# A hybrid decoder block on one core: tiles of f moved by 128 bytes, sums of squares taken on TensorE at three seams, splits of weights ordered behind the root

## The chip, the core and the metric

The kernel runs on one NeuronCore of one Trainium2 chip. The metric is the device time of one execution in microseconds; lower is better. All times below are in us unless they say ns.

## What is computed

One decoder layer over 512 tokens of width 2048, all in float32:

```python
mod = silu(c) @ w_mod + b_mod                    # six vectors: sh1 sc1 gt1 sh2 sc2 gt2
h = rmsnorm(x, g_mix) * (1 + sc1) + sh1
u, q, k, v = split(h @ w_in)                     # 2048 x 4096
y = concat(rmsnorm(s5_mixer(u)), rmsnorm(dilated_attention(q, k, v)))
x = x + gt1 * (y @ w_out)
h = rmsnorm(x, g_ffn) * (1 + sc2) + sh2
f = (silu(h @ w_gate) * (h @ w_up)) @ w_down     # inner width 5632
x = x + gt2 * f
return rmsnorm(x, g_final)

def rmsnorm(x, g):
    return x * rsqrt(mean(x * x, axis=-1) + 1e-6) * g
```

Three of these norms run over the whole width of 2048: before w_in, before w_gate and w_up, and at the end. The change touches how their sums of squares and their roots are formed, and how the last matrix product reads its moving operand.

## The kernel before

**Layout.** Activations are stored transposed, features on the 128 partitions and the 512 tokens along the free dimension, so one tile of a feature block is 128x512 float32, 2048 bytes in a partition. Every matrix product is done as three matmuls in the fp32r format (`mm3`): an operand is split into hi (a cast, on ScalarE) and lo = raw - hi (a subtraction, on VectorE), and hi*hi, hi*lo and lo*hi are accumulated. Weights come by DMA on SP's queue as pieces of 128x1024 (512 KB) into five buffers `raw`; their split goes into three buffers each of `hi` and `lo` (pool `whl`).

**Order.** The kernel is written in a tile framework: the program gives every operation in order, and a planner fixes the order on each engine before the run, from its own estimates and a priority (by default the place in the program; `tc.high_priority(30)` lets an operation go ahead). On the chip each engine, and SP's DMA queue, takes its list strictly in that order. A tile's buffer is taken again when its readers are done. `tc.issue_after(ins)` adds the order "behind ins" for operations on the engine of ins. `prog` is the list of matrix products with calls between them; background generators (`start`, `pump`) put VectorE and ScalarE work between the k steps.

**The head.** x arrives in eight DMAs. Each of its 16 tiles is squared on ScalarE and added on VectorE into `ssq` or `rbc` in turn, and the two are added. Four Silus of c, broadcast over the partitions by matmuls with `sel`, stand between the squares. `rsq_stages` makes the root: four matmuls with a column of ones sum over the partitions (a float32 matmul is two passes, so the profile shows eight), VectorE does a first guess and three Newton steps on a 128x4 tile, four matmuls broadcast the result to 128x512, and it is copied to `rbc`. Meanwhile `gv` multiplies rows of w_mod (512 KB each, eight buffers) with cb, four for each k of the modulation; `h_mod(k)` and `h_make(k)` then make the hi and lo tiles of h (hA for k below 4, hB above). The first product, `first_h` before each of its steps, starts as soon as h(0) is there.

**The seam before gate and up.** `residual(cb_, half)` adds the last quarter of y @ w_out to x1. Each tile is squared on ScalarE and added to ssq on VectorE (`sumsq4`); after the last quarter the root follows (`rsq_psum`), and `h3` makes the two operands b of the next product. `wk_prep(k)` splits the weights of its step k; the splits of k = 0 and 1 are in the program right behind the root.

**The down projection and the end.** f goes through DRAM and comes back as tiles of 128x2x512 (hi and lo beside each other) in eight buffers (pool `ft`). Two products of 44 steps each, 24 matmuls to a step, have the weights stationary and f moving. `acc(c)` adds the eight results of a product to x1 and sums squares the same way; `last` makes the root, multiplies and stores.

**Addresses.** SBUF addresses in a partition, modulo 256 bytes, by the memory map of this kernel: hA, hB, vv, ys, raw, hi, lo and st 192; b, t1 to t4 160; f 64 (114496 and on, 4096 apart). The tile `fpad` in front of `ft` has no other use than to shift it.

Of the kernel before, what the change touches and what calls it, by code (L numbers as in the profile page):

```python
# [10 lines left out]
F32 = mybir.dt.float32  # L11
F32R = mybir.dt.float32r
I32 = mybir.dt.int32
AF = mybir.ActivationFunctionType
ALU = mybir.AluOpType

P = 128
S = 512
D = 2048
KT = D // P  # L20
# [25 lines left out]
def hybrid_block(ctx: ExitStack, tc: tile.TileContext, xT, crow, vecs, pos, kc, km, w_mod, w_in, s5a, s5bc,  # L46
                 s5d, w_glu, w_out, w_gate, w_up, w_down, outT):
    nc = tc.nc
    PE, ACT, DVE, POOL, SP = nc.tensor, nc.scalar, nc.vector, nc.gpsimd, nc.sync
    tt = DVE.tensor_tensor  # L50
    stt = DVE.scalar_tensor_tensor
# [27 lines left out]
    def gps(tag="g"):  # L79
        return banks[tag].tile([P, S], F32, tag=tag, name=nm(tag))  # L80

    def mps():
        return gps("m" if "m" in banks else "g")

    def st():
        return stg.tile([P, S], F32, tag="st", name=nm("st"))
# [5 lines left out]
    bgs = []  # L92

    def start(gen, rate):
        bgs.append([gen, rate, 0.0])
        return bgs[-1]
# [16 lines left out]
    def finish(h):  # L113
        while h in bgs:
            advance(h, 1)
# [115 lines left out]
    ones = kct[:, K_ONE:K_ONE + 1]  # L231
# [3 lines left out]
    cb = const.tile([P, D], F32, name="cb")  # L235
    macc = const.tile([P, 96, 2], F32, name="macc")
    gs = const.tile([P, 16], F32, name="gs")
# [37 lines left out]
    def xf(k):  # L275
        return (vg if k < 8 else xb)[:, k % 8]
# [3 lines left out]
    crow4 = crow_sb[0:4]  # L280
# [28 lines left out]
    def gv(n):  # L309
        for _ in range(n):  # L310
            gv_loads()
            m, h = gq[gat[0]]
            raw = graw.pop(gat[0])
            stt(raw, raw, 1.0, cb[:, h * (D // 2):(h + 1) * (D // 2)], op0=ALU.mult, op1=ALU.mult,  # L314
                accum_out=macc[:, m, h:h + 1])
            gat[0] += 1
            gv_loads()
# [19 lines left out]
    def sumsq(acc, x, first):  # L337
        if first:
            ACT.activation(acc, x, AF.Square)
        else:  # L340
            t = st()
            ACT.activation(t, x, AF.Square)
            tt(acc, acc, t, op=ALU.add)

    def sumsq4(acc, xs, first):

        ts = []
        for i, x in enumerate(xs):
            ts.append(acc if first and i == 0 else st())
            ACT.activation(ts[-1], x, AF.Square)  # L350
        yield
        for t in ts:
            if t is not acc:
                tt(acc, acc, t, op=ALU.add)

    root = [None]

    def rsq_stages(out, acc, n):

        ps = mps()  # L360
        for j in range(4):
            PE.matmul(ps[:, j:j + 1], acc[:, j * P:(j + 1) * P], ones, start=True, stop=True)
        yield
        v = small.tile([P, 4], F32, tag="rv", name=nm("rv"))
        ii = small.tile([P, 4], I32, tag="ri", name=nm("ri"))
        h = small.tile([P, 4], F32, tag="rh", name=nm("rh"))
        t = small.tile([P, 4], F32, tag="rt", name=nm("rt"))
        DVE.tensor_scalar(v, ps[:, :4], 1.0 / n, EPS, op0=ALU.mult, op1=ALU.add)
        DVE.tensor_scalar(ii, v.bitcast(I32), 1, None, op0=ALU.logical_shift_right)
        DVE.tensor_scalar(ii, ii, -1, 0x5F3759DF, op0=ALU.mult, op1=ALU.add)  # L370
        DVE.tensor_scalar(h, v, -0.5, None, op0=ALU.mult)
        y = ii.bitcast(F32)
        for _ in range(3):
            tt(t, y, y, op=ALU.mult)
            tt(t, t, h, op=ALU.mult)
            stt(y, t, 1.5, y, op0=ALU.add, op1=ALU.mult)
        yield
        pb = mps()
        for j in range(4):
            PE.matmul(pb[:, j * P:(j + 1) * P], y[:, j:j + 1].to_broadcast([P, P]), ident,  # L380
                      start=True, stop=True)
        yield
        if out is None:
            root[0] = pb
        else:
            ACT.copy(out, pb)

    def rsq_psum(acc, n):
        for _ in rsq_stages(None, acc, n):
            pass  # L390
        return root[0]

# [80 lines left out]
    gv_loads()  # L473
    gb1 = const.tile([P, 16], F32, name="gb1")
    stt(gb1, vec[:, V_BMOD + SC1:V_BMOD + SC1 + 16], 1.0, vec[:, V_GMIX:V_GMIX + 16], op0=ALU.add, op1=ALU.mult)
    for i in range(KT):
        sumsq((ssq, rbc)[i % 2], xf(i), i < 2)
        if i in (3, 5, 7, 9):
            j = i // 2 - 1
            ps = gps()  # L480
            PE.matmul(ps, sel[:, j], crow4, start=True, stop=True)
            ACT.activation(cb[:, j * S:(j + 1) * S], ps, AF.Silu)
    tt(ssq, ssq, rbc, op=ALU.add)

    def h_mod(k):

# [7 lines left out]
    def h_make(k, between=None):  # L494

        made.add(k)
        hi, lo = act_h(k)
        sh = mod[:, SH1 + k:SH1 + k + 1]
        t = st()
        halves = [slice(0, S // 2), slice(S // 2, S)]  # L500
        for c in halves:
            stt(t[:, c], xf(k)[:, c], gs[:, k:k + 1], rbc[:, c], op0=ALU.mult, op1=ALU.mult)
            ACT.activation(hi[:, c], t[:, c], AF.Identity, bias=sh)
        if between is not None:
            between()
        for c in halves:
            stt(lo[:, c], t[:, c], sh, hi[:, c].bitcast(F32), op0=ALU.add, op1=ALU.subtract)
# [32 lines left out]

    def first_h(k, hi, lo):
        if k == 0:
            rs = rsq_stages(rbc, ssq, D)
            next(rs)
            gv(1)
            next(rs)
            next(rs)
            gv(3)
            h_mod(0)
            for _ in rs:  # L550
                pass
            hi()
        else:
            hi()
            gv(4)
            h_mod(k)
        h_make(k, lo)

    for i, (c0, kg) in enumerate(QK1):
        gemm(wiv, QC + c0, 0, range(kg), act_h, store([part[c0 // P + m] for m in range(8)], SP), w=2 * S,  # L560
# [359 lines left out]
    x1 = []  # L920
# [66 lines left out]
    def attention():  # L987
        with tc.tile_pool(name="att", bufs=2, side="right", reuse_waits="tile") as ap, \
# [83 lines left out]

            yield from pipe(range(4 * NH), a0, a1, a2, a2b, a3, a4, a5)

    def residual(cb_, half):
        def fn(pss):
            assert ('mod', GT1) in made
            fs_ = range(4 * cb_, 4 * cb_ + 4)
            for m, f in enumerate(fs_):
                stt(pss[m], pss[m], mod[:, GT1 + f:GT1 + f + 1], (rbc, ssa)[half], op0=ALU.mult, op1=ALU.mult)  # L1080
                if m:
                    tt(x1[0][:, f - 1], pss[m - 1], x1[0][:, f - 1], op=ALU.add)
            tt(x1[0][:, f], pss[3], x1[0][:, f], op=ALU.add)
            if half:
                SP.dma_start(x1v[:, fs_[0]:f + 1], x1[0][:, fs_[0]:f + 1])
                start(sumsq4(ssq, [x1[0][:, f] for f in fs_], cb_ == 0), 1)
                if cb_ == 3:
                    finish(bgs[-1])
        return fn

    def win5():
# [37 lines left out]
    fd = dram.tile([FF // P, P, 2 * S], F32, name="fd")  # L1129
    finish(hh[-1])  # L1130

    def hl(raw):
        hi = whl.tile([P, 2 * S], F32R, tag="hi", name=nm("hi"))
        lo = whl.tile([P, 2 * S], F32R, tag="lo", name=nm("lo"))
        ACT.copy(hi, raw)  # L1135
        tt(lo, raw, hi.bitcast(F32), op=ALU.subtract)  # L1136
        return hi, lo

    wk, wkr = {}, {}
# [10 lines left out]
                SP.dma_start(v[:, j, i], w[i, kh, :, :, kk * P:(kk + 1) * P].rearrange("f p c -> p f c"))  # L1150
        wkr[k] = t

    def wk_prep(k):
        for j in range(4):
            wk_load(k + j)
        if k < KT:
            with tc.high_priority(30):
                wk[k] = hl(wkr[k])

    for k in range(4):  # L1160
        wk_load(k)
    r = rsq_psum(ssq, D)
    wk_prep(0)
    wk_prep(1)
    yx.close()
    mrx.close()
    open_banks(g=8)
# [170 lines left out]
    def acc(c):  # L1338
        def fn(pss):
            assert ('mod', GT2) in made  # L1340
            xs = [x1[0][:, 8 * c + m] for m in range(8)]
            for m, x in enumerate(xs):
                o = GT2 + 8 * c + m
                stt(x, pss[m], mod[:, o:o + 1], x, op0=ALU.mult, op1=ALU.add)
                if m % 4 == 3:
                    start(sumsq4(ssq, xs[m - 3:m + 1], c == 0 and m == 3), 1)
                    if c == 1:
                        finish(bgs[-1])
        return fn

    gq += [(GT2 + k, h) for k in range(KT) for h in range(2)]
# [13 lines left out]
    for n, (bl, p) in enumerate(items):  # L1365
        prep(n + 2)
        if n == len(items) - 4:

            t12x.close()
            ftx.enter_context(tc.tile_pool(name="fpad", bufs=1, side="right")).tile([P, 24], F32, name="fpad")  # L1370
            fpool = ftx.enter_context(tc.tile_pool(name="ft", bufs=8, side="right", reuse_waits="tile"))
            ft.append(fpool)
            for j in range(7):
                f_load(j)
            while at[1] < 3:
                load_piece(pieces[at[1]])
                at[1] += 1
# [64 lines left out]
    def last():  # L1442
        ov = kview(outT)
        x, g = x1[0], vec[:, V_GFIN:V_GFIN + KT]
        r = rsq_psum(ssq, D)
        for k in range(KT):
            stt(x[:, k], x[:, k], g[:, k:k + 1], r, op0=ALU.mult, op1=ALU.mult)
            SP.dma_start(ov[:, k], x[:, k])
# [78 lines left out]
```

## Time and profile before

| | us |
|---|---|
| median of three runs | 2206.57 (2206.29 to 2213.41) |
| the profiled execution | 2206.05 |
| its span, first to last instruction | 2204.3 |
| first matmul of the first large product | starts at 32.68 |
| product before gate and up ends, first b matmul | 791.8 and 804.37 |
| down projection, first to last matmul | 1691.2 to 2182 |

A line of a timeline shows the start, the duration, the engine, the line of the kernel, the operation with its output and inputs, and in brackets how long the engine was idle before it and what ended that. A line of a table of stretches gives the stretch, its length, then for PE, PEld, DVE, ACT and POOL the busy time with the number of instructions, and at the end the granted TensorE clock, the share of the DMA engines and GB/s. PE is the matmuls, PEld the loading of weights beside them, DVE is VectorE, ACT is ScalarE, SPq is SP's DMA queue.

### The profile page before, as it was taken

The page shows a single profiled execution, that of the slowest core. Times are in us where ns is not written, and L with a number is a line of the kernel's source. Part 1 is how long each engine was busy: PE and PEld are TensorE (multiplying, and loading weights), DVE is VectorE, ACT ScalarE, POOL GpSimd, SP SyncE. Part 2 cuts the span into 40 slices and gives each one's busy share as a digit, 9 for nine tenths or more (in the row PEclk, how much of TensorE's full clock was granted, in tenths as well). Part 3 has the DMA queues.
Part 4 walks back from the last instruction along what each step waited for, and adds up shares of the span by engine and source line. Part 5 has one row for each costly group of instructions (what it writes and reads, how often), then busy time and mean ns, then how long its engine had stood idle before and what let it go on. Part 6 is the DMA issues. An engine that isn't in the chain of part 4 may idle for free.

```text
span 2204.3 us, 32293 instructions
## 1 busy us (share of the span) xinstructions
PE 2114.6 (96%) x12744; PEld 1870.0 (85%) x12744; DVE 1518.0 (69%) x2219; ACT 851.1 (39%) x1213; POOL 2.0 (0%) x7
## 2 busy tenths in 40 slices
PE   5999999889999989999999999999999999999996
PEld 3778787777787868999999999999999888888885
DVE  7896877976888776787887878878886443232225
ACT  3432343366653353444444444444443111121111
POOL 0000000000000000000000000000000000000000
PEclk9999989999999989999999999999999999999998
DMA  9999885678887633343343434434346888555552
GB/s 356 331 355 168 226 265 182 235 232 271 299 280 242 208 105 96 134 144 125 128 140 126 147 121 135 144 125 142 117 140 242 314 320 312 190 189 186 188 171 77
DMA packets 212047, 435.91 MB, mean 198 GB/s; under 512 B 50676, under 2 KB 87924, under 8 KB 211896
## 3 DMA queue, kind: packets, MB, share of 16 engines
q1 hardware_dynamic: 211656, 433.13, 59.3%
q8 instruction: 100, 1.64, 0.3%
q0 software_dynamic: 240, 0.72, 0.1%
q14 instruction: 51, 0.42, 0.1%
HBM read 380.38 MB, written 53.41 MB: 197 GB/s over the span
## 4 chain that ended last, share of the span: by engine, by line
PE 73%; DVE 7%; DMA 4%; issue 1%; ACT 0%; SPq 0%; DVEq 0%; ACTq 0%
PE g L191 11%; PE g L193 11%; PE g L192 11%; PE y L1395 5%; PE y L1393 5%; PE y L1394 5%; PE z L1395 3%; PE x L1395 3%; PE x L1394 3%; PE z L1394 3%; PE z L1393 3%; PE x L1393 3%; DMA mraw<-in_w_mod 3%; DVE mraw L314 1%; PE m L772 1%
## 5 line engine op out<-in xcount | busy, mean ns | idle before, releaser
L165 DVE TENSOR_TENSOR lo<-raw,hi 128x1024 fp32r<-128x1024 f32 x192 | 234.7, 1224 | 336.7 <-ACT hi L161 332.3
L161 ACT CAST hi<-raw 128x1024 fp32r<-128x1024 f32 x192 | 201.2, 1049 | 575.0 <-PE g L192 383.1
L1135 ACT CAST hi<-raw 128x1024 fp32r<-128x1024 f32 x176 | 185.2, 1052 | 290.4 <-PE x L1394 116.6
L314 DVE SCALAR_TENSOR_TENSOR mraw<-mraw,cb 128x1024 f32<-128x1024 f32 x192 | 233.0, 1222 | 80.2 <-DMA mraw<-in_w_mod 80.0
L1136 DVE TENSOR_TENSOR lo<-raw,hi 128x1024 fp32r<-128x1024 f32 x176 | 215.2, 1223 | 94.9 <-ACT hi L1135 94.8
L191 PE MATMUL g<-f,hi 128*128 128x512 f32 x704 | 277.8, 395 | 0.0
L192 PE MATMUL g<-f,hi 128*128 128x512 f32 x704 | 277.8, 395 | 0.0
L193 PE MATMUL g<-f,lo 128*128 128x512 f32 x704 | 277.8, 395 | 0.0
L1135 ACT CAST hi<-s 128x1024 fp32r<-128x1024 f32 x120 | 126.3, 1052 | 165.8 <-PE y L1394 82.6
L1394 PE MATMUL x<-b,hi 128*128 128x256 f32 x640 | 179.8, 281 | 0.0
L1393 PE MATMUL y<-t,hi 128*128 128x256 f32 x640 | 179.8, 281 | 0.0
L1395 PE MATMUL x<-b,lo 128*128 128x256 f32 x640 | 179.8, 281 | 0.0
L1394 PE MATMUL y<-t,hi 128*128 128x256 f32 x640 | 179.8, 281 | 0.0
L1395 PE MATMUL y<-t,lo 128*128 128x256 f32 x640 | 179.8, 281 | 0.0
L1393 PE MATMUL x<-b,hi 128*128 128x256 f32 x640 | 179.8, 281 | 0.0
L191 PEld LDWEIGHTS g<-f,hi 128*128 128x128 f32 x704 | 132.6, 188 | 31.0
L192 PEld LDWEIGHTS g<-f,hi 128*128 128x128 f32 x704 | 132.6, 188 | 30.9
L193 PEld LDWEIGHTS g<-f,lo 128*128 128x128 f32 x704 | 132.6, 188 | 30.9
L1136 DVE TENSOR_TENSOR lo<-s,hi 128x1024 fp32r<-128x1024 f32 x120 | 146.4, 1220 | 16.8 <-ACT hi L1135 16.3
L191 PE MATMUL g<-hB,hi 128*128 128x512 f32 x288 | 115.6, 403 | 12.6 <-DVE rt L883 12.5
L1394 PEld LDWEIGHTS x<-b,hi 128*128 128x128 f32 x640 | 120.6, 188 | 0.0
L1393 PEld LDWEIGHTS x<-b,hi 128*128 128x128 f32 x640 | 120.6, 188 | 0.0
(312 smaller groups left out, 4928.5 us busy)
## 6 DMA issues: line engine op xcount, KB each, us to landing
mraw<-in_w_mod SPq DMA_DIRECT2D x192, 512.0 KB, 6.1
raw<-in_w_down SPq DMA_DIRECT2D x88, 512.0 KB, 4.1
f<-fd SPq DMA_DIRECT2D x88, 512.0 KB, 3.9
raw<-in_w_gate SPq DMA_DIRECT2D x80, 512.0 KB, 3.3
raw<-in_w_up SPq DMA_DIRECT2D x80, 512.0 KB, 3.7
raw<-in_w_in SPq DMA_DIRECT2D x64, 512.0 KB, 5.4
fd<-fo SPq DMA_DIRECT2D x40, 512.0 KB, 4.4
raw<-in_w_out SPq DMA_DIRECT2D x32, 512.0 KB, 5.5
```

The source lines that it names most:

```text
L161: ACT.copy(hi, p["raw"])
L165: tt(p["hl"][1], p["raw"], p["hl"][0].bitcast(F32), op=ALU.subtract)
L191: PE.matmul(ps, lhs[0], rhs[0], start=first, stop=False)
L192: PE.matmul(ps, lhs[0], rhs[1], start=False, stop=False)
L193: PE.matmul(ps, lhs[1], rhs[0], start=False, stop=last)
L314: stt(raw, raw, 1.0, cb[:, h * (D // 2):(h + 1) * (D // 2)], op0=ALU.mult, op1=ALU.mult, accum_out=macc[:, m, h:h + 1])
L772: PE.matmul(d["pi"][:, i * NJ:(i + 1) * NJ], d["pm"][i // 4][:, i % 4], Ug[:, 8 * c + i], start=True, stop=True)
L1135: ACT.copy(hi, raw)
L1136: tt(lo, raw, hi.bitcast(F32), op=ALU.subtract)
L1393: PE.matmul(o, hi[:, sl], bh[:, k], start=f, stop=False, skip_group_check=True)
L1394: PE.matmul(o, hi[:, sl], bo[:, k], start=False, stop=False, skip_group_check=True)
L1395: PE.matmul(o, lo[:, sl], bh[:, k], start=False, stop=l, skip_group_check=True)
```

## The change

In the head the four Silus come ahead of the squares; one square in four is done on VectorE; four tiles' squares are added into a tile of their own, and this tile goes to TensorE's sum over partitions (`ssq_mm`), which accumulates the four groups in one PSUM tile. The root is taken ahead of the four products of w_mod for k = 0, which are put behind the last Newton step; h(0) reads the root from PSUM, and the copy to `rbc` comes after h(0). In `residual` and `acc` the last two squares skip the add into ssq and go to TensorE by themselves. The lo parts of the split weights for k = 0 and 1 are put behind the last add to x1 and behind the last Newton step. `fpad` has 56 floats in place of 24.

```diff
-    def rsq_stages(out, acc, n):
-
-        ps = mps()
+    chain = [None]
+    def ssq_mm(ps, x, first, last):
         for j in range(4):
-            PE.matmul(ps[:, j:j + 1], acc[:, j * P:(j + 1) * P], ones, start=True, stop=True)
+            PE.matmul(ps[:, j:j + 1], x[:, j * P:(j + 1) * P], ones, start=first and j == 0, stop=last,
+                      skip_group_check=True)
+    def rsq_stages(out, acc, n, ps=None):
+        if ps is None:
+            ps = mps()
+            for j in range(4):
+                PE.matmul(ps[:, j:j + 1], acc[:, j * P:(j + 1) * P], ones, start=True, stop=True)
...
-            stt(y, t, 1.5, y, op0=ALU.add, op1=ALU.mult)
+            chain[0] = stt(y, t, 1.5, y, op0=ALU.add, op1=ALU.mult)
...
+        root[0] = pb
         yield
-        if out is None:
-            root[0] = pb
-        else:
+        if out is not None:
             ACT.copy(out, pb)
...
+    psx = gps()
+    for j in range(4):
+        ps = gps()
+        PE.matmul(ps, sel[:, j], crow4, start=True, stop=True)
+        ACT.activation(cb[:, j * S:(j + 1) * S], ps, AF.Silu)
     for i in range(KT):
-        sumsq((ssq, rbc)[i % 2], xf(i), i < 2)
-        if i in (3, 5, 7, 9):
-            j = i // 2 - 1
-            ps = gps()
-            PE.matmul(ps, sel[:, j], crow4, start=True, stop=True)
-            ACT.activation(cb[:, j * S:(j + 1) * S], ps, AF.Silu)
-    tt(ssq, ssq, rbc, op=ALU.add)
+        q = st()
+        if i % 4 == 2:
+            tt(q, xf(i), xf(i), op=ALU.mult)
+        else:
+            ACT.activation(q, xf(i), AF.Square)
+        if i % 4:
+            tt(acc4, acc4, q, op=ALU.add)
+        else:
+            acc4 = q
+        if i % 4 == 3:
+            ssq_mm(psx, acc4, i == 3, i == KT - 1)
...
-            stt(t[:, c], xf(k)[:, c], gs[:, k:k + 1], rbc[:, c], op0=ALU.mult, op1=ALU.mult)
+            stt(t[:, c], xf(k)[:, c], gs[:, k:k + 1], (rbc if k else root[0])[:, c], op0=ALU.mult, op1=ALU.mult)
...
         if k == 0:
-            rs = rsq_stages(rbc, ssq, D)
+            rs = rsq_stages(rbc, None, D, psx)
+            with tc.high_priority(30):
+                next(rs)
+                next(rs)
             next(rs)
-            gv(1)
-            next(rs)
-            next(rs)
-            gv(3)
+            with tc.issue_after(chain[0].ins):
+                gv(4)
             h_mod(0)
-            for _ in rs:
-                pass
             hi()
...
         h_make(k, lo)
+        if k == 0:
+            for _ in rs:
+                pass
...
             if half:
+                x1_done[:] = [done]
                 SP.dma_start(x1v[:, fs_[0]:f + 1], x1[0][:, fs_[0]:f + 1])
-                start(sumsq4(ssq, [x1[0][:, f] for f in fs_], cb_ == 0), 1)
-                if cb_ == 3:
-                    finish(bgs[-1])
+                if cb_ < 3:
+                    sq.append(start(sumsq4(ssq, [x1[0][:, f] for f in fs_], cb_ == 0), 1))
+                    return
+                for h in sq:
+                    finish(h)
+                psq.append(mps())
+                ts = []
+                for f in fs_:
+                    ts.append(st())
+                    ACT.activation(ts[-1], x1[0][:, f], AF.Square)
+                for t in ts[:2]:
+                    tt(ssq, ssq, t, op=ALU.add)
+                for i, t in enumerate((ssq, *ts[2:])):
+                    ssq_mm(psq[0], t, i == 0, i == 2)
...
+        with tc.issue_after(after.ins) if after is not None else nullcontext():
+            tt(lo, raw, hi.bitcast(F32), op=ALU.subtract)
...
-    r = rsq_psum(ssq, D)
-    wk_prep(0)
-    wk_prep(1)
+    with tc.high_priority(30):
+        r = rsq_psum(None, D, psq[0])
+    wk_prep(0, x1_done[0])
+    wk_prep(1, chain[0])
...
-                if m % 4 == 3:
-                    start(sumsq4(ssq, xs[m - 3:m + 1], c == 0 and m == 3), 1)
-                    if c == 1:
-                        finish(bgs[-1])
+                if c == 0:
+                    if m % 4 == 3:
+                        start(sumsq4(ssq, xs[m - 3:m + 1], m == 3), 1)
+                else:
+                    ts.append(st())
+                    ACT.activation(ts[m], x, AF.Square)
+                    if m < 6:
+                        tt(ssq, ssq, ts[m], op=ALU.add)
+            if c == 1:
+                psq[0] = mps()
+                for i, t in enumerate((ssq, *ts[6:])):
+                    ssq_mm(psq[0], t, i == 0, i == 2)
...
-            ftx.enter_context(tc.tile_pool(name="fpad", bufs=1, side="right")).tile([P, 24], F32, name="fpad")
+            ftx.enter_context(tc.tile_pool(name="fpad", bufs=1, side="right")).tile([P, 56], F32, name="fpad")
```

More of the change, by code (lines that the diff above doesn't have):

```diff
@@ L381, in rsq_stages, with rsq_psum @@
                       start=True, stop=True)
+        root[0] = pb
         yield
-        if out is None:
-            root[0] = pb
-        else:
+        if out is not None:
             ACT.copy(out, pb)
-    def rsq_psum(acc, n):
-        for _ in rsq_stages(None, acc, n):
+    def rsq_psum(acc, n, ps=None):
+        for _ in rsq_stages(None, acc, n, ps):
             pass
@@ L1073, in attention @@
             yield from pipe(range(4 * NH), a0, a1, a2, a2b, a3, a4, a5)
+    sq, psq, x1_done = [], [], []
     def residual(cb_, half):
@@ L1082, in fn @@
                     tt(x1[0][:, f - 1], pss[m - 1], x1[0][:, f - 1], op=ALU.add)
-            tt(x1[0][:, f], pss[3], x1[0][:, f], op=ALU.add)
+            done = tt(x1[0][:, f], pss[3], x1[0][:, f], op=ALU.add)
             if half:
+                x1_done[:] = [done]
                 SP.dma_start(x1v[:, fs_[0]:f + 1], x1[0][:, fs_[0]:f + 1])
-                start(sumsq4(ssq, [x1[0][:, f] for f in fs_], cb_ == 0), 1)
-                if cb_ == 3:
-                    finish(bgs[-1])
+                if cb_ < 3:
[12 more added lines that the diff above has]
+                    ssq_mm(psq[0], t, i == 0, i == 2)
         return fn
@@ L1130, in hybrid_block, with hl @@
     finish(hh[-1])
-    def hl(raw):
+    def hl(raw, after=None):
         hi = whl.tile([P, 2 * S], F32R, tag="hi", name=nm("hi"))
@@ L1135, in hl @@
         ACT.copy(hi, raw)
-        tt(lo, raw, hi.bitcast(F32), op=ALU.subtract)
+        with tc.issue_after(after.ins) if after is not None else nullcontext():
+            tt(lo, raw, hi.bitcast(F32), op=ALU.subtract)
         return hi, lo
@@ L1151, in wk_load, with wk_prep @@
         wkr[k] = t
-    def wk_prep(k):
+    def wk_prep(k, after=None):
         for j in range(4):
@@ L1157, in wk_prep @@
             with tc.high_priority(30):
-                wk[k] = hl(wkr[k])
+                wk[k] = hl(wkr[k], after)
     for k in range(4):
         wk_load(k)
-    r = rsq_psum(ssq, D)
-    wk_prep(0)
-    wk_prep(1)
+    with tc.high_priority(30):
+        r = rsq_psum(None, D, psq[0])
+    wk_prep(0, x1_done[0])
+    wk_prep(1, chain[0])
     yx.close()
@@ L1341, in fn @@
             xs = [x1[0][:, 8 * c + m] for m in range(8)]
+            ts = []
             for m, x in enumerate(xs):
@@ L1444, in last @@
         x, g = x1[0], vec[:, V_GFIN:V_GFIN + KT]
-        r = rsq_psum(ssq, D)
+        r = rsq_psum(None, D, psq[0])
         for k in range(KT):
```

## The prediction

> **What bounds the kernel now.** I read the page's busy list first, then the busy time of stretches that hold only matmuls, then the chain of work that ended last at the two late root computations, then the order of time in the first 60 us.
>
> ```profile
> span 2204.3 us, 32293 instructions
> PE 2114.6 (96%) x12744; PEld 1870.0 (85%) x12744; DVE 1518.0 (69%) x2219; ACT 851.1 (39%) x1213; POOL 2.0 (0%) x7
> ...
> 120.00:220.00 100.00, 100.00 (x442) 82.79 (x442) 78.05 (x175) 28.49 (x39) 1.20 (x2) 1.00 0.99 249
> 840.00:880.00 40.00, 40.00 (x173) 32.21 (x172) 20.52 (x14) 12.47 (x11) 0.00 (x0) 1.00 0.34 105
> 1700.00:1900.00 200.00, 200.00 (x862) 162.13 (x861) 82.72 (x102) 37.75 (x36) 0.00 (x0) 1.00 0.84 298
> 1940.00:2140.00 200.00, 200.00 (x863) 162.13 (x862) 45.22 (x38) 37.72 (x36) 0.00 (x0) 1.00 0.57 192
> ...
> L191 PE MATMUL g<-f,hi x704: 390/393/404, 1691.2 to 2181.3; 128*128 128x512 f32 x176
> ```
>
> TensorE is busy 96% of the span, so time can come from two places only: a shorter step between matmuls, or a shorter hole. The four stretches have PE full at a granted clock of 1.00, and their matmuls stream 512 columns. A matmul that straddles an edge is counted on both sides, so I take one off each count: 100/441 = 0.2268 us where hA and hB are streamed, 40/172 = 0.2326 for b, 200/861 = 0.2323 and 200/862 = 0.2320 in f's two halves. The share of the DMA engines (next to last column) is 0.99 in the quick stretch, and f's pace is the same at 0.84 and at 0.57: traffic is not the reason. The f row gives the pace over the whole stage: 703 triples between its first and last start, 490.1 us, so 5.577 us for the 24 matmuls of one k.
>
> **Term A, the tiles of f.** The pad in front of them grows from 24 to 56 floats, so they move 128 bytes down, from 64 to 192 modulo 256. In the kernel's memory map hA, hB, vv and ys stand at 192, the weights' hi and lo also, b at 160. The gemm over vv has the shape of the down projection (weights stationary, 512 contiguous floats moving); its pace is the distance of two splits, each of which follows the matmuls of one k:
>
> ```profile
> 775.36 1.05 ACT L161 CAST hi<-raw 128x1024 fp32r<-128x1024 f32 x1 [2.65 <-PE g L192]
> 780.80 1.05 ACT L1135 CAST hi<-raw 128x1024 fp32r<-128x1024 f32 x1 [4.39 <-DMA raw<-in_w_up]
> ```
>
> That is 5.44 us, and 24 x 0.2268 gives 5.44 as well. If f at 192 runs as these do, 88 steps (704 triples, 8 to a step) save 88 x (5.577 - 5.44) = 12.1 us. Nothing else holds the stage: PE has no hole in it, and the DMA share of 0.84 would rise to 0.86. Bounds: 12.1 (no row is quicker than 5.44) and nothing (the offset is not the cause); a loss is priced among the rivals. I take 12.1, since every 512-column tile at 192 has that pace. [...]
>
> **Term B, the root before the gate and up projections.** The last matmul, then the chain of waits:
>
> ```profile
> 791.43 0.39 PE L193 MATMUL g<-vv,lo 128*128 128x512 f32 x1
> ...
> 791.40 1.23 DVE lo L1136
> 792.63 0.67 DVE g L1080
> 793.80 0.69 DVE x L1083
> 794.49 1.13 DVE lo L1136
> 795.62 0.61 DVE ssq L354
> 796.37 1.85 PE m L362 x8
> 800.73 2.06 PE m L380 x8
> 802.81 0.76 DVE st L1185
> 803.60 0.73 ACT b L1188
> 804.37 0.79 PE g L191
> ...
> 794.52 0.63 ACT L350 ACTIVATE st<-x 128x512 f32<-128x512 f32 x1 [1.70 <-DVE x L1083]
> ...
> 578.72 0.79 PE m L362 x8
> ...
> 586.04 0.89 PE m L380 x8
> ```
>
> Two splits (lo) stand in this chain ahead of the root, and an add into ssq follows the last square. The change holds the split of k = 0 until x1 is done, that of k = 1 until the Newton chain is done, and gives the last two squares to TensorE directly. New sum from the last matmul's end at 791.82: g 0.67, x 0.69, square 0.63 and 0.1 of hand-over make 793.9. The sums over ssq and the third square run meanwhile, behind the last matmul: 8 passes cost 0.79 on a busy PE (row 578.72), two sets end at 793.4, so both are hidden; at the cold price of 1.85 they would end at 795.5. The set for the last square costs 0.79 to 1.85; I take 1.05, which the same work took 2.3 us after the last matmul in the tail (below): 795.0. Newton's 2.5 (796.37 + 1.85 to 800.73) makes 797.5, the broadcast 2.06, st 0.76, b 0.73: first matmul 801.1 instead of 804.37, so 3.3. The split of k = 0 lies under the square and the sum (1.1 of 1.8 us), that of k = 1 under the broadcast (1.1 of 2.06); uncovered each costs 1.13. The split of k = 2 has no such edge and can still slip in ahead of Newton, so I take 3.0. Bounds: all three sets cold, 791.82 + 3 x 1.85 = 797.4 against 798.2, gain 0.8; the last set at 0.79, gain 3.6. On SP the store of x1 waits for x1 and has loads of weights behind it; both come earlier, and those weights are for k of 2 and more, 11 us on.
>
> [...]
>
> **Term C, the last root.**
>
> ```profile
> 2181.92 0.25 PE g L193
> 2182.19 0.76 DVE x L1344
> 2183.04 0.64 ACT st L350
> 2183.70 0.70 DVE ssq L354
> 2184.45 1.07 PE g L362 x8
> 2187.93 2.09 PE g L380 x8
> ```
>
> The add (0.70 and 0.05 of hand-over) goes. The sets for ssq and the seventh square run from 2182.17: at 0.79 they end at 2183.75, just when the eighth square is there (2183.70), and the whole 0.75 plus 0.28 of a warmer last set is won; at 1.07 they end at 2184.3 and 0.15 is left. Taken: 0.7. The sixteen outputs behind it stay.
>
> **Term D, the head.**
>
> ```profile
> 3.63 7.19 PE L481 MATMUL g<-st,st 4*128 4x512 f32 x8 [3.63 <-DVE st L469]
> 15.16 3.23 ACT L342 ACTIVATE st<-xb 128x512 f32<-128x512 f32 x6
> 18.85 0.68 DVE L343 TENSOR_TENSOR rbc<-rbc,st 128x512 f32<-128x512 f32 x1
> 20.71 4.19 SPq L305 DMA_DIRECT2D mraw<-in_w_mod  x3
> 21.34 1.87 PE L362 MATMUL g<-kct,ssq 128*128 128x1 f32 x8 [10.51 <-DVE ssq L483]
> 27.91 2.08 PE L380 MATMUL g<-kct,ri 128*128 128x128 f32 x8 [4.71 <-DVE ri L376]
> 30.06 1.22 DVE L314 SCALAR_TENSOR_TENSOR mraw<-mraw,cb 128x1024 f32<-128x1024 f32 x1
> 31.21 0.48 DVE L502 SCALAR_TENSOR_TENSOR st<-vg,gs,rbc 128x256 f32<-128x256 f32 x1
> 32.68 0.79 PE L191 MATMUL g<-hA,hi 128*128 128x512 f32 x1 [2.69 <-ACT hA L503]
> 43.70 0.79 PE L193 MATMUL g<-hA,lo 128*128 128x512 f32 x1 [2.68 <-DVE lo L165]
> 51.27 1.23 DVE L165 TENSOR_TENSOR lo<-raw,hi 128x1024 fp32r<-128x1024 f32 x1 [3.02 <-ACT hi L161]
> ```
>
> All four Silus now stand ahead of the squares; the broadcast they read ends at 10.8, so ACT may start its 12 squares at 11.4 and end them at 18.3 (0.57 each), as before (18.4). DVE has 16 operations at 0.60 in place of 15, and its last add ends between 17.5 (x streams in freely) and 21.5 (nothing of it done before 11.4); taken 19.5. Then sums 1.87, Newton 2.5, and only then the four products with w_mod, 4 x 1.15, and 0.4 of small ones: h(0) starts at 28.9 instead of 31.21, and the first matmul 2.3 earlier. But DVE is the bound here, and before the change two more products and a split (3.45 us) were done by 31.21. With them it is 32.3, so DVE runs 1.1 late, and the next wait of PE, at 43.70, is for DVE: what is won at k = 0 is waited out at k = 1. What DVE loses meets its 3.02 us of idling at 51.27. SP reloads w_mod 4 to 5 us later than 20.71, with w_in behind; eight products' worth of tiles is in flight by then, which covers it to about 26. PSUM: the root's bank, read by h(0) directly, is freed by the copy to rbc one step later, before the eighth bank is asked for. Bounds: 3 won, 3 lost; taken: 0.5 won.
>
> **Sum.** 12.1 + 3.0 + 0.7 + 0.5 = 16.3 us off the profiled execution's 2206.05 (1.75 more than its span; 0.52 below the median of the runs, 2206.57): 2189.8.
>
> **Rivals.**
> 1. *The offset does not matter to f* (its tiles are DMA-written, which hA and vv are not). For it: b at 160 and f at 64 differ by 0.1% only. Against: weights, which feed the same matmuls, never change. 2206.05 - 4.2 = 2201.9; Chance 0.10. [...]
> 2. *The head loses.* stg has five buffers; if each group's sum tile is handed on only after its PE sums, a group takes 1.87 + 0.57 + 3 x 0.60 = 4.2 us in series, the last add ends at 14.3 + 12.7 = 27.0, h(0) starts at 36.4, 5.2 late. 2189.8 + 0.5 + 5.2 = 2195.5. Against: two tiles free up at 10.8 and leave all five. Chance 0.11.
> 3. *192 is the wrong residue for f*: moving operand and weights then start alike, and f has eight tiles where vv has one block. Price from the 256-column matmuls at 160:
>
> ```profile
> 960.00:1000.00 40.00, 40.00 (x340) 40.00 (x339) 32.39 (x37) 18.11 (x23) 0.00 (x0) 1.00 0.40 133
> ```
>
> 40/339 = 0.1180 each, 0.2360 for 512 columns, 5.66 us for a step: 88 x 0.087 = 7.6 lost, 2206.05 + 7.6 - 4.2 = 2209.5, slower. It decides from 5.625 us for a step on. Against: hA to ys, all alike with the weights. Chance 0.04.
> 4. *PE stays warm at the seam of term B*: the broadcast 1.2 shorter, eight matmuls at 0.23 in place of 0.43 (1.6): 2187.0. Against: the tail's 2.09. Chance 0.08. [...]
>
> **Numbers.** My forecast keeps 0.67. About 0.3% (6.6 us) is what a measurement of this kernel can tell from no change. Faster by more than that (below 2199.4): forecast, rival 4 and nearly all of rival 2, 0.85; within: rival 1 and the near part of rival 3, 0.12; slower 0.03. Range: below, 2189.8 - 2.5 (head) - 1.1 (B and C at their best) - 2.2 (most of rival 4) = 2184; above, rival 2 with B at its lower bound, 2195.5 + 2.2 = 2197.7, 2198. It leaves out rivals 1 and 3.
>
> **What would show it.** Right: the f row spans 478 to 479 us, with mean durations of 389 to 391 ns; the first b matmul starts 9.5 us after the last vv matmul's end in place of 12.6; the last Newton chain follows the square without an add. Wrong: an f step of 5.58 (rival 1) or above 5.62 (rival 3); a PE wait in the first 60 us longer than those at 32.68 and 43.70 together; a split between x1 and Newton.

## The result and the profile after

| | before | after |
|---|---|---|
| median of the runs | 2206.43 (2206.13 to 2213.41, four runs) | 2189.8 (2189.05 to 2192.96, four runs) |
| profiled execution, its span | 2206.05, 2204.3 | 2189.05, 2187.2 |

The ratio is 0.9914, with an interval of 0.9895 to 0.9933. The comparison leaves out disturbed runs.

The busy list of the kernel after, then its stretches that hold only matmuls (columns as before), then the row of f:

```profile
span 2187.2 us, 32392 instructions
PE 2109.8 (96%) x12800; PEld 1874.8 (86%) x12800; DVE 1516.8 (69%) x2216; ACT 849.6 (39%) x1209; POOL 2.0 (0%) x7
```

```profile
840.00:880.00 40.00, 40.00 (x173) 32.20 (x172) 16.19 (x12) 9.16 (x9) 0.00 (x0) 1.00 0.34 105
1700.00:1900.00 200.00, 200.00 (x884) 165.59 (x883) 81.34 (x101) 39.04 (x37) 0.00 (x0) 1.00 0.86 301
```

```profile
L191 PE MATMUL g<-f,hi x704: 389/389/396, 1686.5 to 2164.5; 128*128 128x512 f32 x176
```

TensorE holds f's stretch without a gap as before, but with 884 matmuls in place of 862: 200/883 = 0.2265 us. The f row spans 478.0 in place of 490.1; over its 703 triples that is 0.2266 a matmul in place of 0.2324. The gemm over b, which was not moved, is at 173 in its 40 us as before.

The seam before gate and up, on TensorE's timeline and then in the chain of waits:

```profile
788.86 0.39 PE L193 MATMUL g<-vv,lo 128*128 128x512 f32 x1
789.08 0.95 PE L362 MATMUL m<-kct,ssq 128*128 128x1 f32 x8
789.89 1.03 PE L362 MATMUL m<-kct,st 128*128 128x1 f32 x8
791.49 1.05 PE L362 MATMUL m<-kct,st 128*128 128x1 f32 x8 [0.56 <-ACT st L1116]
795.06 2.04 PE L388 MATMUL m<-kct,ri 128*128 128x128 f32 x8 [2.52 <-DVE ri L384]
798.79 0.79 PE L191 MATMUL g<-b,hi 128*128 128x512 f32 x1 [1.68 <-ACT b L1222]
```

```profile
790.08 0.70 DVE x L1103
790.80 0.64 ACT st L1116
791.49 1.07 PE m L362 x8
795.15 0.95 issue
796.10 1.22 DVE lo L1169
797.32 0.67 DVE st L1219
```

From the last matmul's end (789.25) to the first b it is 9.54 in place of 12.55. The two sums that need not wait stand right behind the last matmul, the third follows the last square, and a split appears in the chain only behind the Newton steps (lo at 796.10, which runs beside the broadcast and ends 0.2 behind it: 797.32 against 795.06 + 2.04).

The tail, TensorE's timeline, then ScalarE's last square:

```profile
2164.98 0.39 PE L193 MATMUL g<-f,lo 128*128 128x512 f32 x1
2165.45 1.05 PE L362 MATMUL g<-kct,ssq 128*128 128x1 f32 x8
2166.37 1.93 PE L362 MATMUL g<-kct,st 128*128 128x1 f32 x16
2170.73 2.08 PE L388 MATMUL g<-kct,ri 128*128 128x128 f32 x8 [2.43 <-DVE ri L384]
```

```profile
2166.25 0.63 ACT L1385 ACTIVATE st<-x 128x512 f32<-128x512 f32 x1 [0.73 <-DVE x L1379]
```

Three sets now run in a row, 2.85 us from 2165.45, in place of a single one behind an add. From the start of the last matmul the span ends 22.22 us later, before the change 22.52 (2204.27 - 2181.76). In the experiments below it is 22.09 to 22.45 with this tail.

The head, first TensorE, then VectorE:

```profile
20.62 1.86 PE L362 MATMUL g<-kct,st 128*128 128x1 f32 x8 [1.36 <-DVE st L495]
24.92 2.08 PE L388 MATMUL g<-kct,ri 128*128 128x128 f32 x8 [2.43 <-DVE ri L384]
33.45 1.65 PE L191 MATMUL g<-hA,hi 128*128 128x512 f32 x3 [6.45 <-ACT hA L519]
```

```profile
28.22 1.22 DVE L314 SCALAR_TENSOR_TENSOR mraw<-mraw,cb 128x1024 f32<-128x1024 f32 x1
29.50 1.22 DVE L165 TENSOR_TENSOR lo<-raw,hi 128x1024 fp32r<-128x1024 f32 x1
30.83 1.22 DVE L314 SCALAR_TENSOR_TENSOR mraw<-mraw,cb 128x1024 f32<-128x1024 f32 x1
31.97 0.87 DVE L518 SCALAR_TENSOR_TENSOR st<-vg,gs,g 128x256 f32<-128x256 f32 x2
```

The root is ready 3 us earlier (broadcast at 24.92 in place of 27.91), but h(0) (L518) starts at 31.97, later than the 31.21 of before: behind the four products VectorE does the split of the first weights and a fifth product. The first large matmul starts at 33.45 in place of 32.68.

Summed along TensorE, the profiled pair differs by: up to the last matmul of the product over vv 2.6 earlier, the hole before b 3.0 shorter, gemm over b 0.8 longer, f 12.0 shorter, tail 0.3 shorter; 17.1 in all.

### The profile page after: what moved, and what is told of

Read it like the earlier page. It is cut to its first block, busy times and chain, and to the rows that moved or that the text cites. A ratio compares the mean times of both kernels' runs of the same rounds, so it can differ in the third digit from the quotient of the medians.

```text
span 2187.2 us, 32392 instructions
## 1 busy us (share of the span) xinstructions
PE 2109.8 (96%) x12800; PEld 1874.8 (86%) x12800; DVE 1516.8 (69%) x2216; ACT 849.6 (39%) x1209; POOL 2.0 (0%) x7
## 4 chain that ended last, share of the span: by engine, by line
PE 73%; DVE 8%; DMA 3%; issue 1%; ACT 0%; DVEq 0%; SPq 0%; ACTq 0%
PE g L191 11%; PE g L193 11%; PE g L192 11%; PE y L1436 5%; PE y L1437 5%; PE y L1438 5%; PE z L1437 3%; PE x L1437 3%; PE x L1436 3%; PE z L1436 3%; PE x L1438 3%; PE z L1438 3%; DMA mraw<-in_w_mod 3%; DVE mraw L314 1%; DVE lo L165 1%
## 5 line engine op out<-in xcount | busy, mean ns | idle before, releaser
L191 PE MATMUL g<-f,hi 128*128 128x512 f32 x704 | 273.9, 389 | 0.0
L192 PE MATMUL g<-f,hi 128*128 128x512 f32 x704 | 273.9, 389 | 0.0
L1169 DVE TENSOR_TENSOR lo<-s,hi 128x1024 fp32r<-128x1024 f32 x120 | 146.5, 1221 | 16.3 <-ACT hi L1167 15.7
```

The lines of the kernel that those rows point to most:

```text
L191: PE.matmul(ps, lhs[0], rhs[0], start=first, stop=False)
L192: PE.matmul(ps, lhs[0], rhs[1], start=False, stop=False)
```

## The experiments

Where a figure is called "last vv" it is the start of the last matmul of the product before gate and up, "first hB" the first matmul of the product on hB, "hole" the time from the last vv matmul's end to the first b matmul.

**f alone.**

```diff
 # kernel before
-ftx.enter_context(tc.tile_pool(name="fpad", ...)).tile([P, 24], F32, name="fpad")
+ftx.enter_context(tc.tile_pool(name="fpad", ...)).tile([P, 56], F32, name="fpad")
```

> The kernel before with only the pad in front of f's tiles grown from 24 to 56 floats (f at 192 modulo 256 bytes). Theory (the start address sets the pace): the f row spans 478.0 us instead of 490.1, mean durations 389 instead of 390 to 393 ns, and the rest of the trace stays where it was: 2206.4 - 12.1 = 2194.3. Rival (the quicker f stage needs the earlier or shorter seams of the whole change, for instance another phase of its loads): the row stays at 490 us and the time at 2206.

Measured: 2199.83 against 2210.06, ratio 0.9957 (0.9942 to 0.9972), that is 6 to 13 us.

```profile
L191 PE MATMUL g<-f,hi x704: 389/389/395, 1696.1 to 2174.2; 128*128 128x512 f32 x176
```

478.1 from first to last: the pad alone gives the 12.0. But the row begins at 1696.1, in the kernel before at 1691.2, though up to there both run the same instructions in the same order. Executions of one program differ by 5 us on the way; the 6.4 us that the kernel after had seemed to win between 490 and 790 us have to be judged against that.

**The head alone, and everything but the head.**

```diff
 # head_only: the kernel before with the head of the kernel after
 # head_undone: the kernel after with this in place of its head
+        sumsq((ssq, rbc)[i % 2], xf(i), i < 2)
+        if i in (3, 5, 7, 9):
+            ...                      # one of the four Silus
+    tt(ssq, ssq, rbc, op=ALU.add)
...
+            rs = rsq_stages(rbc, ssq, D)      # gv(1), gv(3) and the copy to rbc ahead of h(0)
```

> The kernel before with only the head changed (squares in groups of four, summed over partitions by TensorE, all Silus first, the root read from PSUM). Theory 1 (the head's later start brings the 6.4 us back in the middle): first matmul with hA at 33.4, the last matmul with vv 2.6 us earlier than before, time 2203.8. Theory 2 (the head only costs): the last matmul with vv 3.8 us later, time 2210.2. Theory 3, that of the prediction's sum: 2205.9.

> The kernel after with the head of the kernel before (sixteen squares on ScalarE in two sums, the four Silus in between, products with w_mod around the root). In the kernel after, TensorE is 3.8 us later than before at 490 us and has won 6.4 us between there and the seam at 790, in instructions of unchanged order. Theory 1 (those 6.4 us are an echo of the head: the later start lets loads and attention meet in another phase): both go, and the time is 2189.0 + 2.6 = 2191.7, first matmul of the gemm over b back at about 802. Theory 2 (the 6.4 us come from elsewhere and the head simply costs 3.8): first matmul of the gemm over b at 795, time 2185.2.

Measured: head_only 2208.28 against 2210.06, ratio 0.9994 (0.998 to 1.0008); head_undone 2195.08, ratio 0.9941 (0.992 to 0.9961). The positions, first those of head_undone, then those of head_only:

```profile
L191 PE MATMUL g<-hB,hi x288: 387/389/774, 84.9 to 485.4; 128*128 128x512 f32 x144
L193 PE MATMUL g<-vv,lo x192: 387/389/499, 496.3 to 794.2; 128*128 128x512 f32 x192
```

```profile
L191 PE MATMUL g<-hB,hi x288: 387/389/792, 90.5 to 489.3; 128*128 128x512 f32 x144
L193 PE MATMUL g<-vv,lo x192: 387/389/501, 498.7 to 796.3; 128*128 128x512 f32 x192
```

With the head of before (three traces: before, f_only, head_undone) first hB lies at 84.9 to 85.3 and last vv at 791.4, 793.7 and 794.2, mean 793.1. With the head of after (seven traces that differ elsewhere only from the seam on: after, head_only, splits_free, and below b_at_192, f_at_0, f_at_160, residues) first hB lies at 88.4 to 90.5, mean 89.3, and last vv at 788.0 to 797.9, mean 793.2. So the head costs 4 us in the first 90 us, and 700 us later nothing of it is left; what takes it up was not followed. Of the 4 us, 0.8 is the later first matmul. One of TensorE's waits for hA is longer in the kernel after (3.67 us at 58.60 in place of 1.94 at 57.71), and the granted clock from the first hA to the first hB is lower: 0.97 in the three traces with the head of before, 0.94 in four and 0.91 in three of the seven with that of after. Those at 0.94 reach hB at 88.4 to 89.1, those at 0.91 at 89.8 to 90.5. Both theories that I had set against each other fall: neither does the head bring the 6.4 us, nor does its cost last. head_undone, which has every other part of the change, gains 15.0 us (2210.06 - 2195.08). The 788.9 of the kernel after is at the quick end of a spread of 10 us.

**The seam without the two orders.**

```diff
 # kernel after
-    wk_prep(0, x1_done[0])
-    wk_prep(1, chain[0])
+    wk_prep(0)
+    wk_prep(1)
```

> The kernel after without the two orders that hold the splits of k = 0 and k = 1 back (the squares still go to TensorE, the root still has the higher priority). Theory 1 (the orders matter): both splits stand ahead of the Newton chain on VectorE again, 1.2 us each, of which the first lies partly beside the square and the sums: the hole between the last matmul with vv and the first with b grows from 9.5 to 10.7 to 12.0 us, time 2190.2 to 2191.5. Theory 2 (the root's priority alone keeps them behind): hole 9.5, time 2189.0.

Measured: 2194.54, ratio 0.9933 (0.9916 to 0.995). The chain:

```profile
794.25 0.75 DVE g L1100
795.01 1.12 DVE lo L1169
796.77 0.64 ACT st L1116
797.45 1.88 PE m L362 x8
801.84 2.06 PE m L388 x8
...
805.48 0.79 PE g L191
```

The hole is 11.95. Theory 1 holds, but the splits do their harm ahead of x: the one at 793.11 (1.23 us) puts g off by 0.7, the one at 795.01 goes between g and x, and together they put the last sum off by 1.7 us (3.92 behind the last matmul's end, with the orders 2.24). The sum itself costs 1.88 in place of 1.07: it ran at a granted clock of 0.50, that of the kernel after at 1.00. Both make about the 2.4 us between the two holes. The squares on TensorE are then worth 12.55 - 11.95 = 0.6 by themselves. The hole is 12.55 in before, f_only and head_only and 9.54 in after and head_undone. Of the ten traces with both orders, here and below, seven have 9.54; the other three are taken up with h0_first.

**Which place of f is quick.**

```diff
 # kernel after
-... .tile([P, 56], F32, name="fpad")
+... .tile([P, 40], F32, name="fpad")      # f_at_0;   f_at_160: [P, 64]
```

> The kernel after with f at 0 modulo 256 bytes. Theory 1 (192 alone is quick, or only what agrees with the weights, which stand at 192): 5.577 us a step or more, f row 490 us, about +12. Theory 2 (64 alone is slow): 5.44, f row 478.

> The kernel after with f at 160 modulo 256 bytes, where b stands. Theory 1 (the pace of b, 0.2326, is due to its address): f row about 491 us, time +12. Theory 2 (b's pace is due to its two runs of 256 columns): f row 478 us, time unchanged.

The f rows, f_at_0 first, then f_at_160:

```profile
L191 PE MATMUL g<-f,hi x704: 396/397/398, 1696.9 to 2189.0; 128*128 128x512 f32 x176
```

```profile
L191 PE MATMUL g<-f,hi x704: 394/396/397, 1685.0 to 2177.1; 128*128 128x512 f32 x176
```

492.1 both, slower than at 64 (490.1); times 2213.39 and 2201.51 in one run each, apart by the scatter of the stages before. Of four places 192 alone is quick, the place where the weights stand. Theory 1 holds in both runs: f at 160 takes 0.2333 us a matmul (492.1 / 703 / 3), and so does b, which stands there too. In the kernel after, 171 matmuls over b lie between the starts at 840.13 and 880.02. The counts of stretches had put b at 0.2326: a record (0.39 us) outlasts a step, so that a stretch of 40 us counts more than one matmul too many.

**Weights moved to where f was.**

```diff
 # kernel after, fpad back at 24 (f at 64)
+    ctx.enter_context(tc.tile_pool(name="wpad", bufs=1)).tile([P, 32], F32, name="wpad")
     whl = ctx.enter_context(tc.tile_pool(name="whl", bufs=3, reuse_waits="tile"))
```

> The kernel after with f back at 64 and a pad of 128 bytes ahead of the split weights, which brings them (and the tiles behind them on that side) from 192 to 64 modulo 256 bytes; hA, hB, vv and ys stay at 192. Theory 1 (the moving operand's own address sets the pace): hA and hB still 0.2268 us a matmul, f 0.2323, f row 490 us, time about 2201. Theory 2 (weights and moving operand must agree modulo 256): f row 478 us, and the gemms over hA, hB, vv and ys, some 2500 matmuls, lose 0.0055 us each, 14 us: about 2203.

One run, 2201.89. The row of f and the stretch over hA and hB:

```profile
L192 PE MATMUL g<-f,hi x704: 389/389/401, 1699.4 to 2177.5; 128*128 128x512 f32 x176
```

```profile
120.00:220.00 100.00, 100.00 (x432) 80.89 (x431) 79.74 (x178) 28.30 (x39) 1.19 (x2) 1.00 0.99 260
```

f stays at 64 and is quick (478.1); hA and hB stay at 192 and are now slow, 100/431 = 0.2320. So theory 2: with the places taken modulo 256 bytes, f and hA are quick in these runs (0.2266 to 0.2268) where they start as the weights do, and slow (0.2320 to 0.2333) at the other places tried. That the pattern repeats every 256 bytes was not tested by itself; no run moved a tile by 256. The expected 14 us in the other gemms did not show: last vv is at 790.3, inside the spread, though each 100 us there hold ten matmuls fewer. What took up the rest was not followed. What the run loses against the kernel after lies in the 256-column products, whose weights moved too: 12.3 us (807.8 from the last b to the first f matmul, against 795.5).

The pace differs by the pair of places, not by either place alone: (weights 192, moving 192) 0.2266, (192, 64) 0.2324, (64, 192) 0.2320, (64, 64) 0.2267, by the f rows (478.0, 490.1 and 478.1 over 703 triples) and the stretch. No run here shows what part of the chip makes the pace depend on the pair.

**b and t1 to t4 on the same place.**

```diff
 # kernel after; fpad 64, so that f stays at 192
-    bp.tile([P, 8], F32, name="bpad")
```

> The kernel after with the 32-byte pad behind b taken away, so that b and t1 to t4 stand at 192 modulo 256 bytes in place of 160; f stays at 192 (its pad grows by 32 bytes). Theory 1 (192 is quick for every moving operand): the gemm over b goes from 0.2326 to 0.2268 us a matmul, 384 x 0.0058 = 2.2 us; the 256-column products from 0.1180 to half of 0.2268, 0.1134, some 6700 x 0.0046 = 31 us: 2156. Theory 2 (in these two stages the reads go in runs of 256 columns and the start address is not what costs): both paces stay, 2189. Theory 3 (160 was the better place for 256 columns): slower.

Measured: 2203.05 against 2206.68, ratio 0.9972 (0.9959 to 0.9986): slower than the kernel after.

```profile
840.00:880.00 40.00, 40.00 (x179) 33.10 (x178) 19.62 (x14) 11.04 (x9) 0.00 (x0) 1.00 0.34 103
960.00:1000.00 40.00, 40.00 (x336) 40.00 (x335) 31.75 (x37) 18.08 (x23) 0.00 (x0) 1.00 0.38 129
```

The gemm over b gets quicker, with 179 matmuls in the 40 us in place of 173. By the starts (176 matmuls from 840.08 to 879.97) it is at 0.2267, the pace of f at 192, where it was at 0.2333. The 256-column products get slower: 336 in place of 340 in the same stretch, 0.1200 by the starts where they took 0.1183, and with it 807.7 us from the last b to the first f matmul against 795.5. Theory 3: what suits 512 columns does not suit 256.

**Four places for the 256-column products in one run.**

```diff
 # kernel after
-    bp.tile([P, 8], F32, name="bpad")
+    bp.tile([P, 16], F32, name="bpad")        # b 64 below the weights
+            pool.tile([P, dict(t4=16, t1=8, t2=16)[n]], F32, name=f"pad{n}")
```

> The kernel after with pads that put the moving operands of the 256-column products at four places against their weights, which stay at 192 modulo 256 bytes: b at 128 (64 below), t4 (now qd) at 64 (128 off), t1 (qa) at 224 (32 above), t2 (qb) at 0 (64 above); f stays at 192. Measured so far for 256 columns: 0.1182 us at 32 below, 0.1199 at 0 and at 96 below. Theory 1 (256 columns have one quick place, 32 below, and the rest are alike): all seven products 0.1199 us a matmul, mean duration 283 ns, about 11 us more than after. Theory 2 (a place nearer the ideal exists, as agreement is for 512 columns): at least one of the four below 0.1182, mean duration under 281 ns. The gemm over b at 64 below: 0.2326 or more (theory: only agreement is quick), f 0.2265.

One run, 2184.87. The groups of three of the products:

```profile
L1437 PE MATMUL y<-qd,hi 128*128 128x256 f32 x320 | 90.4, 282 | 0.7 <-DVE u L1462 0.6
L1437 PE MATMUL z<-qa,hi 128*128 128x256 f32 x320 | 89.2, 279 | 0.0
L1437 PE MATMUL y<-b,hi 128*128 128x256 f32 x320 | 88.5, 277 | 0.0
```

In the kernel after every one of these groups has 281. Here they run from 276 (y<-b, 64 below) to 282 (128 off), and 784.3 us pass from the last b to the first f matmul, 11.2 less. Theory 2. One place gave two paces, though: z<-b, also at 64 below, is at 281. And x<-b, at the same place, takes 0.1133 us a matmul when it follows y<-b and, in 35 of 39 cases, 0.1178 when it follows z<-b, which stands behind the product over qd. So the pace hangs on what ran just before as well. The gemm over b stays slow at 64 below (92.0 us from its first matmul to its last, 92.2 in the kernel after).

**h(0) ahead of the fifth product.**

```diff
 # kernel after
+            with tc.high_priority(60):
                 with tc.issue_after(chain[0].ins):
                     gv(4)
                 h_mod(0)
...
+        with nullcontext() if k else tc.high_priority(60):
             for c in halves:             # first half of h_make
```

> The kernel after with a higher priority for the four products with w_mod of k = 0, h_mod(0) and the first half of h_make(0), which takes the fifth product (1.22 us) out from between them on VectorE; the split of the first weights stays ahead of h(0). Theory 1 (the prediction's step: h(0) and the first matmul come earlier, and the gain is waited out at k = 1, VectorE being the bound of the head): first matmul at 32.2 in place of 33.45, first matmul with hB at 88 to 91 as before, time unchanged (2189). Theory 2 (what the planner put ahead of h(0) is what made the head dearer): the first matmul with hB 1.2 us earlier too, at about 88.4 (mean of the three runs with this head: 89.6), time 1.2 less.

Measured: 2191.55 against 2207.37, ratio 0.9931 (0.9908 to 0.9953).

```profile
32.25 1.65 PE L191 MATMUL g<-hA,hi 128*128 128x512 f32 x3 [5.31 <-ACT hA L520]
```

The first matmul comes 1.2 earlier, as set out. First hB is at 86.4 here and at 88.8 and 89.8 in the two runs below, which have this head too; mean 88.3, against 88.4 to 90.5 without it. The clock has a part in this scatter: it is 0.97 up to first hB here, 0.91 in the two others. At 0.91 the two reach hB at 89.3 in the mean, the three with the head of after at 90.3, which speaks for theory 2 but rests on five traces. By last vv (789.4) nothing of it could be seen.

This run also has a hole of 10.36 with the same instructions. Its third sum, then the clock of that sum, here and (last line) in the kernel after:

```profile
792.03 1.87 PE L362 MATMUL m<-kct,st 128*128 128x1 f32 x8 [0.56 <-ACT st L1118]
```

```profile
792.03:793.90 1.87, 1.87 (x8) 1.78 (x8) 0.42 (x1) 0.00 (x0) 0.00 (x0) 0.50 0.90 338
791.49:792.54 1.05, 1.05 (x8) 0.96 (x8) 0.41 (x1) 0.00 (x0) 0.00 (x0) 1.00 0.80 302
```

In both traces the third sum starts 2.24 us behind the last vv matmul's end, but here the granted clock is down to 0.50 by then, and the sum takes 1.87 in place of 1.05. That is the 0.8 us; everything behind it follows at the same distances. f_at_0 has the same (hole 10.35, sum 1.86 at 0.50), and in w_at_64 the clock falls during the sum (0.72 over it, sum 1.35, hole 9.84). In the fourteen traces the clock falls between 2.0 and 5.2 us behind the last vv matmul's end; no run shows what sets the moment. So of the 2.4 us of the two orders, about 1.7 comes from the splits, and about 0.8 depends on the clock still being up when the last sum runs.

**All of b and t1 to t4 at 128, and at 96.**

```diff
 # h0_first
-    bp.tile([P, 8], F32, name="bpad")
+    bp.tile([P, 16], F32, name="bpad")        # bt_at_128, fpad 48;  bt_at_96: 24, fpad 40
```

> The kernel after with b and t1 to t4 all at 128 modulo 256 bytes (64 below the weights), f at 192, and h(0) ahead of the fifth product on VectorE. In the run with four places the products over b at 128 took 0.1138 to 0.1175 us a matmul, against 0.1184 in the kernel after, the quickest of them (y<-b) not behind a product with another place. Theory 1 (a place counts for each product by itself and 0.1138 is that of 64 below; the slower ones were held up by their neighbours): 6720 x 0.0046 = 31 us less between the gemm over b and the one over f, with the head's 1.2: about 2157. Theory 2 (it is the change of place from product to product, or the accumulation, that decides): 0.1155 as the mean over b there, 6720 x 0.0029 = 19 us less: 2168. The gemm over b stays at 0.2326.

> The same with b and t1 to t4 at 96 modulo 256 bytes (96 below the weights). With the weights at 64 and b and t at 160, 96 above, the pace was 0.1199. Theory 1 (the pace gets quicker the further below the weights the moving operand starts): at or under the pace at 128, so at most 2157. Theory 2 (64 below is the one quick place): 0.1184 to 0.12, 2188 to 2200.

Measured: bt_at_128 2181.36 against 2208.09, ratio 0.9881 (0.9857 to 0.9906), the quickest of all here; bt_at_96 2189.8 in one run. Two stretches of bt_at_128, and from the timeline the longest wait of TensorE in this stage, which lies between them:

```profile
1060.00:1100.00 40.00, 40.00 (x355) 40.00 (x354) 34.01 (x38) 18.45 (x25) 0.00 (x0) 1.00 0.43 147
1200.00:1240.00 40.00, 40.00 (x342) 40.00 (x341) 32.35 (x37) 18.09 (x24) 0.00 (x0) 1.00 0.40 133
```

```profile
1160.68 0.36 PE L1438 MATMUL y<-t,hi 128*128 128x256 f32 x1 [1.02 <-ACT hi L1169]
```

Up to this wait of 1.0 us the 24 matmuls of a product take 2.72 us, 0.1133 each by their starts; behind it they take 2.83, 0.1178 each, and it stays so to the end of the stage. Addresses, instructions and the clock (1.00) are the same. So neither theory holds: the place alone does not set the pace of 256 columns. The two paces are those that x<-b had in turn in the run with four places. Nor does a wait alone change it: in f_only, with b and t1 to t4 32 below the weights, a wait of 1.27 us at 1192.89 leaves the pace at 0.1183. The gemm over b stays slow, as both theories had it (91.7 us). At 96 the same happens on a smaller scale (343 matmuls in the earlier stretch, 339 in the later). The stage takes 783.2 us against 795.5, so this version is 12 us quicker there than the kernel after; the two were not run side by side, and their intervals overlap. Whether the pace of 0.1133 can be kept through the stage was not tried.

## Why the prediction was right, and where it was not

The time was predicted at 2189.8 and measured at 2189.8, the sum at 16.3 and by the stages that repeat at 12.0 + 3.0 + 0.3 = 15.3, where the medians differ by 16.6. The agreement to 0.1 us is luck: executions of one program differ by several us (2206.13 to 2213.41 before the change).

- **Term A** (12.1): 12.0, shown by the pad alone. The step of 5.44 and the absence of any other bound held. The reason given was wrong in part: 192 is quick where the weights stand there too (0.2266), and with the weights at 64 it takes 0.2320. Rival 3, by which a like start of both would be slow, has the sign reversed for 512 columns; for 256, from which its price was taken, 192 is in fact slower than 160 (0.1200 against 0.1183). The paces from counts of stretches were some 0.3% too short: b at 160 takes 0.2333, so b and f at 64 differ by 0.4% and not by the 0.1% that rival 1 leaned on.
- **Rival 1** fell with the f row of f_only.
- **Term B** (3.0): 3.0, of which the two orders make 2.4 and the sums on TensorE 0.6. The last set took 1.07 (taken: 1.05), but that hangs on the clock: in two of ten traces it took 1.86 and 1.87 and the gain was 2.2, inside the bounds of 0.8 to 3.6. Behind Newton the splits end 0.2 after the broadcast, which is about the 0.3 that had been kept. A split does stand between x1 and Newton, that of k = 0, under the last square and its sum, where this term had put it.
- **Rival 4** is out. The broadcast of the seam took 2.04 behind waits of 0.56 and 2.52 (row at 795.06), the next matmul 0.79: TensorE was slow again, at a granted clock of 0.50 in the broadcast and in the matmuls from 798.79 to 804. No run here shows the broadcast of 0.89 or the steps of 0.23 at this seam, from which the 2187.0 and the 2.2 in the range were taken; the broadcast took 2.04 in before and after, and the first steps over b 0.43 (805.75 on in before, 800.16 on in after). The 0.8 us by which the profiled execution's gemm over b is longer is no steady cost: head_undone, with the same seam, takes 91.43 for it where before has 91.40.
- **Term C** (0.7): 0.3. Mis-sized was the price of a set: 0.79, that of a busy TensorE, was taken for the two early ones, and all three took 0.95 (2.85 together). The row at 578.72 counts its set from the end of the matmul before it; on the timeline the same set starts at 578.56 and takes 0.95. They end at 2168.30, 1.4 us behind the eighth square (2166.25 + 0.63): the sums, not the square, were last.
- **Term D** (0.5): by the means of last vv nothing, 0.1 the other way, within a spread of 10. The size held, the steps did not. VectorE's order was taken from the program (four products, then h(0)); the planner put a split and a fifth product ahead of h(0), 2.5 us, and the first matmul came 0.8 later in place of 2.3 earlier. The row that was to tell this came: a wait of 6.45 in the first 60 us, more than the 2.69 and 2.68 of before together. That the difference is evened out at k = 1 did not come: it grew from 0.8 to 4 us at first hB, by a longer wait and a lower clock, and is gone only at 790. That VectorE is the bound of the head was not tested by itself. Of rival 2 a little appears, ScalarE's squares waiting 0.47 and 1.29 us for TensorE's sums, far from its 5.2.

## What to carry over

Where a matmul stage is full and its clock is at 1.00, work out the pace per matmul and compare it between stages, from starts rather than from counts where a few tenths of a per cent matter; a few ns that stay with a stage (0.2324 against 0.2266 us here) can be the distance of two addresses, and a pad of some floats tests it. Test it for each number of columns by itself, since what gained 12 us at 512 columns lost 12 at 256. And before a difference of a few us in one pair of traces is explained, compare a stage that both kernels run alike: here it alone moved by 5 to 10 us. Look at the granted clock of the instruction too: the same sum at the same distance from the work before it took 1.05 or 1.87 us.

## What the hardware showed that was not expected

- The pace of 512-column fp32r matmuls changed with where the moving operand starts against the weights, both places taken modulo 256 bytes: 0.2266 us at the same place, 0.2324 at 128 off, 0.2333 (492.1 / 703 / 3) at 64 above and at 32 below. The gemm over b follows it: 0.2267 at the same place, 0.2333 at 32 below.
- With 256 columns and the moving operand 64 bytes below the weights, the same addresses gave 0.1133 and 0.1178 us in one execution, and a single wait of 1.0 us stood between the two paces for good. At 32 below it was 0.1183, at the same place and at 96 above 0.1200, throughout.
- The 4-column sums behind the 512-column matmuls took 0.95 to 1.07 at a granted clock of 1.00 and 1.84 to 1.88 at 0.50. The clock fell 2.0 to 5.2 us behind the last 512-column matmul at the seam. In the kernel after, sums ran in between, and TensorE's longest wait there was 2.52 us.
